# Rotating 96 images by 90 degrees: loads in 1 MB pieces with 32 KB reads over four partitions, middle stores in 32 KB runs

## The chip, the cores and the metric

The kernel runs on one core of a Trainium2 chip. The metric is the device time of one execution in microseconds. Most executions of a kernel agree within 0.3%; a run over 1.5% above the fastest of its kernel is counted as slow and left out of the comparisons. A ratio is the mean time of one kernel's fast runs over the mean of the other's from the same rounds on the same chip, so it is not quite the ratio of the medians that are quoted.

## The reference

```python
def setup_inputs():
    return {"x": np.random.randn(32, 3, 256, 256).astype(np.float32)}   # 25.17 MB

def reference(x):
    return np.rot90(x, k=1, axes=(-2, -1)).astype(np.float32)
```

Every image is turned by a quarter: 25.17 MB are read and as much is written. There is no arithmetic. VectorE transposes small blocks, and the rest of the rotation lies in the access patterns. SyncE and ScalarE do nothing here but issue transfers, each on a queue of its own (q1 and q10 in the profile); 16 DMA engines carry out both queues.

## The kernel before

The data is cut into 24 pieces of 1 MB (4 images each). The first four and last four pieces are handled one by one, the 16 in the middle in four groups of 4 MB. There are 12 slots of 1 MB (8 KB in each of the 128 partitions) for input (`S_all`) and 12 for output (`U_all`).

```python
    AS = [1] * 4 + [4] * 4 + [1] * 4
    for i, a in enumerate(AS):
        s = n % NS                      # NS = 12 slots
        ...
        eng = nc.scalar if i in (1, 3) else nc.sync
        if a == 1:                      # 1 MB: 128 rows of 8 KB, one in each partition
            eng.dma_start(out=S, in_=xg[n].rearrange("(p f) -> p f", p=P))
        else:                           # 4 MB: 128 rows of 32 KB, one in each partition
            eng.dma_start(out=S, in_=xg[n : n + a].rearrange("a (qk f) -> qk a f", f=RI * W))
        ...                             # 1 or 8 nc.vector.transpose
        # stores, always in runs of 8 KB, on ScalarE's queue
        nc.scalar.dma_start(out=og[n : n + a].rearrange("a (p f) -> p a f", p=P), in_=U)
```

The framework places the semaphores: it hands eight DMA completion semaphores round, and a transfer that reuses one waits until the previous transfer on it has landed.

Of the kernel before, what the change touches and what calls it, by code (L numbers as in the profile page):

```python
# [1 line left out]

# [4 lines left out]


@with_exitstack
def kernel(  # L10
    ctx: ExitStack,
    tc: tile.TileContext,
    x: bass.AP,
    out: bass.AP,
):
    nc = tc.nc
    B, C, H, W = x.shape
    assert H == W == 256
    N = B * C
    P = 128  # L20
    R = 8
    F = R * W
    G = N // 4

    AS = [1] * 4 + [4] * 4 + [1] * 4
    assert sum(AS) == G
    NS = NU = 12
    fp32 = mybir.dt.float32

    xf = x.rearrange("b c h w -> (b c h w)")  # L30
    of = out.rearrange("b c h w -> (b c h w)")
    xg = xf.rearrange("(n f) -> n f", n=G)
    og = of.rearrange("(n f) -> n f", n=G)

    S_all = ctx.enter_context(tc.tile_pool(name="S", bufs=1)).tile([P, NS, F], fp32, name="S_all")
    U_all = ctx.enter_context(tc.tile_pool(name="U", bufs=1)).tile([P, NU, F], fp32, name="U_all")

    n = 0
    for i, a in enumerate(AS):
        s = n % NS  # L40
        assert s + a <= NS
        RI = R * a
        S = S_all[:, s : s + a].rearrange("p a f -> p (a f)")
        U = U_all[:, s : s + a]

        eng = nc.scalar if i in (1, 3) else nc.sync
        if a == 1:
            eng.dma_start(out=S, in_=xg[n].rearrange("(p f) -> p f", p=P))
        else:
            eng.dma_start(  # L50
                out=S, in_=xg[n : n + a].rearrange("a (qk f) -> qk a f", f=RI * W)
            )

        src = S.rearrange("p (r k q) -> p q r k", r=RI, q=R)[:, ::-1, :, ::-1]
        dst = U.rearrange("p a (q k r) -> p q r k a", q=R, r=RI)
        if a == 1:
            nc.vector.transpose(dst[:, :, :, :, 0], src)  # L57
        else:
            for q in range(R):
                nc.vector.transpose(dst[:, q], src[:, q])  # L60

        if a == 1:
            nc.scalar.dma_start(out=og[n].rearrange("(p f) -> p f", p=P), in_=U[:, 0])
        else:
            nc.scalar.dma_start(
                out=og[n : n + a].rearrange("a (p f) -> p a f", p=P), in_=U
            )
        n += a


# [1 line left out]
_INS = ['x']  # L72
_OUTS = [((32, 3, 256, 256), 'float32')]


# [23 lines left out]
```

## Time and profile before

| | before |
|---|---|
| median of 4 runs | 123.59 us (123.52 to 123.69) |
| span in the profile | 121.8 us |
| VectorE busy | 94.3 us, 77% |
| DMA packet time, share of 16 engines | 98.2% |

The page's main lines stand in the prediction. The timeline of VectorE before shows how the groups follow each other; columns are start, length of the stretch, engine, line, operation, and in brackets the idle time before it with what ended it:

```profile
24.97 31.70 DVE L60 STREAM_TRANSPOSE U_all<-S_all 128x1024 f32<-128x1024 f32 x16 [1.30 <-DMA S_all<-in_x_dram]
62.83 15.93 DVE L60 STREAM_TRANSPOSE U_all<-S_all 128x1024 f32<-128x1024 f32 x8 [6.15 <-issue]
79.44 15.93 DVE L60 STREAM_TRANSPOSE U_all<-S_all 128x1024 f32<-128x1024 f32 x8 [0.69 <-DVE U_all L60]
```

The first row holds two 4 MB groups back to back. The third group starts at 62.8 us and the fourth at 79.4 us.

### The profile page before, as it was taken

Reading aid. Unit: us, or ns where it says so; the run is one execution under the profiler, and the core shown is the slowest. Engines: PE = TensorE matmul, PEld = TensorE weight load, DVE = VectorE, ACT = ScalarE, POOL = GpSimd, SP = SyncE. Lnnn points to the kernel's source line nnn. Section 1 sums busy time; section 2 is a strip of 40 time slices with the busy share of each in tenths; the row PEclk is TensorE's granted clock in tenths of the full one; section 3 lists DMA queues with packets and bytes.
Section 4 is the critical chain, followed back from the end, with each engine's and each line's share of the span. In section 5 each row is a group of like instructions: output and inputs, shape, how many; then the busy total and the mean of one; then the engine's idle time right before and its main releaser. Section 6 shows DMA issues by size and latency. Waiting matters only on the chain.

```text
span 121.8 us, 127 instructions
## 1 busy us (share of the span) xinstructions
DVE 94.3 (77%) x40; POOL 0.2 (0%) x4
## 2 busy tenths in 40 slices
DVE  0029999779999999996039999899999999993000
POOL 0000000000000000000000000000000000000000
DMA  4999989899989998999899999999999999999995
GB/s 86 409 422 428 549 355 441 347 503 430 430 358 503 430 430 361 511 441 430 315 431 430 430 430 420 431 428 425 428 425 428 428 425 430 430 430 428 428 430 213
DMA packets 4992, 50.33 MB, mean 413 GB/s; under 512 B 384, under 2 KB 384, under 8 KB 384
## 3 DMA queue, kind: packets, MB, share of 16 engines
q10 hardware_dynamic: 3552, 27.26, 53.2%
q1 hardware_dynamic: 1440, 23.07, 45.0%
HBM read 25.17 MB, written 25.17 MB: 413 GB/s over the span
## 4 chain that ended last, share of the span: by engine, by line
DMA 54%; DVE 35%; DVEq 2%; issue 0%
DMA out_dram<-U_all 47%; DVE U_all L57 25%; DVE U_all L60 10%; DMA S_all<-in_x_dram 6%; DVEq L94 2%
## 5 line engine op out<-in xcount | busy, mean ns | idle before, releaser
L60 DVE STREAM_TRANSPOSE U_all<-S_all 128x1024 f32<-128x1024 f32 x32 | 63.6, 2073 | 8.1 <-issue 6.2
L57 DVE STREAM_TRANSPOSE U_all<-S_all 128x2048 f32<-128x2048 f32 x8 | 30.8, 3925 | 8.2 <-DMA S_all<-in_x_dram 8.2
L83 POOL MEMSET const-bfloat16-1.0<- 128x1 bf16 x1 | 0.1, 102 | 0.0
L83 POOL MEMSET const-uint8-127<- 128x1 uint8 x1 | 0.1, 102 | 0.0
L83 POOL MEMSET const-float32-1.0<- 128x1 f32 x1 | 0.1, 99 | 0.0
L83 POOL MEMSET const-float32-0.0<- 128x1 f32 x1 | 0.1, 98 | 0.2 <-issue 0.2
## 6 DMA issues: line engine op xcount, KB each, us to landing
S_all<-in_x_dram SPq DMA_DIRECT2D x4, 4096.0 KB, 24.4
out_dram<-U_all ACTq DMA_DIRECT2D x4, 4096.0 KB, 28.7
out_dram<-U_all ACTq DMA_DIRECT2D x8, 1024.0 KB, 15.1
S_all<-in_x_dram SPq DMA_DIRECT2D x6, 1024.0 KB, 9.7
S_all<-in_x_dram ACTq DMA_DIRECT2D x2, 1024.0 KB, 9.9
```

The source lines that it names most:

```text
L57: nc.vector.transpose(dst[:, :, :, :, 0], src)
L60: nc.vector.transpose(dst[:, q], src[:, q])
L83: nc = _bacc.Bacc("TRN2", target_bir_lowering=False, num_devices=1)
L94: with _tile.TileContext(nc) as tc:
```

## The change

Its intent: larger runs everywhere. Stores of 16 images write 32 KB runs instead of 8 KB. For that, a partition must hold one 8 KB row of each of the four pieces of a group, so middle loads can no longer put 32 KB into one partition. Instead, each 32 KB read is written to four neighbouring partitions, piece by piece, and the loads are meant to be issued 12 pieces ahead. The core of the diff (cut):

```diff
-            eng.dma_start(
-                out=S, in_=xg[n : n + a].rearrange("a (qk f) -> qk a f", f=RI * W)
+            nc.sync.add_instruction(
+                mybir.InstDMACopy(
+                    ...
+                    ins=[nc.sync.lower_ap(xv[n], opt=False)],          # 32 reads of 32 KB
+                    outs=[nc.sync.lower_ap(S_all[:, s], opt=False)],   # 128 partitions, 8 KB each
+                    queue="qSPDynamicHW",
...
-                out=og[n : n + a].rearrange("a (p f) -> p a f", p=P), in_=U
+            out=og[n : n + m].rearrange("b (qk f) -> qk b f", f=R * m * W), in_=U
...
+    with tc.manual_schedule():
+        loaded = 0
+        n = 0
+        for m in MS:
+            while loaded < min(n + NS, G):      # NS = 12
+                load(loaded, loaded % NS)
+                loaded += 1
+            turn(m, n % NS)
+            store(n, m, n % NS)
+            n += m
```

More of the change, by code (lines that the diff above doesn't have):

```diff
@@ L23 @@
     G = N // 4
-    AS = [1] * 4 + [4] * 4 + [1] * 4
-    assert sum(AS) == G
+    MS = [1] * 4 + [4] * 4 + [1] * 4
+    assert sum(MS) == G
     NS = NU = 12
+    FOLD = 32
     fp32 = mybir.dt.float32
@@ L31 @@
     of = out.rearrange("b c h w -> (b c h w)")
-    xg = xf.rearrange("(n f) -> n f", n=G)
+    xp = xf.rearrange("(n p f) -> n p f", n=G, p=P)
+    xv = xf.rearrange("(n d f) -> n d f", n=G, d=FOLD)
     og = of.rearrange("(n f) -> n f", n=G)
@@ L36, with load @@
     U_all = ctx.enter_context(tc.tile_pool(name="U", bufs=1)).tile([P, NU, F], fp32, name="U_all")
-    n = 0
-    for i, a in enumerate(AS):
-        s = n % NS
-        assert s + a <= NS
-        RI = R * a
-        S = S_all[:, s : s + a].rearrange("p a f -> p (a f)")
-        U = U_all[:, s : s + a]
-        eng = nc.scalar if i in (1, 3) else nc.sync
-        if a == 1:
-            eng.dma_start(out=S, in_=xg[n].rearrange("(p f) -> p f", p=P))
-        else:
-            eng.dma_start(
-                out=S, in_=xg[n : n + a].rearrange("a (qk f) -> qk a f", f=RI * W)
-            )
-        src = S.rearrange("p (r k q) -> p q r k", r=RI, q=R)[:, ::-1, :, ::-1]
-        dst = U.rearrange("p a (q k r) -> p q r k a", q=R, r=RI)
-        if a == 1:
-            nc.vector.transpose(dst[:, :, :, :, 0], src)
-        else:
-            for q in range(R):
-                nc.vector.transpose(dst[:, q], src[:, q])
-        if a == 1:
-            nc.scalar.dma_start(out=og[n].rearrange("(p f) -> p f", p=P), in_=U[:, 0])
-        else:
-            nc.scalar.dma_start(
-                out=og[n : n + a].rearrange("a (p f) -> p a f", p=P), in_=U
-            )
-        n += a
+    def load(n, s):
+        if n in (0, 2):
+            nc.sync.dma_start(out=S_all[:, s], in_=xp[n])
+        elif n in (1, 3):
+            nc.scalar.dma_start(out=S_all[:, s], in_=xp[n])
+        else:
+            nc.sync.add_instruction(
+                mybir.InstDMACopy(
+                    name=nc.get_next_instruction_name(),
+                    engine=mybir.EngineType.SP,
+                    ins=[nc.sync.lower_ap(xv[n], opt=False)],
+                    outs=[nc.sync.lower_ap(S_all[:, s], opt=False)],
+                    queue="qSPDynamicHW",
+                    mode="Copy",
+                )
+            )
@@ new lines, in turn, with store @@
+    def turn(m, s):
+        RO = R * m
+        S = S_all[:, s : s + m]
+        U = U_all[:, s : s + m].rearrange("p m f -> p (m f)")
+        src = S.rearrange("p b (r k q) -> p r q k b", r=R, q=RO)[:, :, ::-1, ::-1]
+        dst = U.rearrange("p (q k r) -> p r q k", q=RO, r=R)
+        if m == 1:
+            nc.vector.transpose(dst, src[:, :, :, :, 0])
+        else:
+            for r in range(R):
+                nc.vector.transpose(dst[:, r], src[:, r])
+    def store(n, m, s):
+        U = U_all[:, s : s + m].rearrange("p m f -> p (m f)")
+        nc.scalar.dma_start(
+            out=og[n : n + m].rearrange("b (qk f) -> qk b f", f=R * m * W), in_=U
+        )
@@ L72 @@
+    with tc.manual_schedule():
[5 more added lines that the diff above has]
+                loaded += 1
+            assert n % NS + m <= NS
+            turn(m, n % NS)
+            store(n, m, n % NS)
+            n += m
 _INS = ['x']
```

## The prediction

> **What bounds the kernel now.** I read the page of the kernel before first for its engine shares, because a pure copy-and-transpose has only two candidates: VectorE and the 16 DMA engines.
>
> ```profile
> DVE 94.3 (77%) x40; POOL 0.2 (0%) x4
> ...
> DMA  4999989899989998999899999999999999999995
> ...
> DMA packets 4992, 50.33 MB, mean 413 GB/s; under 512 B 384, under 2 KB 384, under 8 KB 384
> ...
> q10 hardware_dynamic: 3552, 27.26, 53.2%
> q1 hardware_dynamic: 1440, 23.07, 45.0%
> ```
>
> VectorE is busy 77% of the 121.8 us span. The two DMA queues (q1 is issued by SyncE, q10 by ScalarE) hold 53.2 + 45.0 = 98.2% of what 16 engines have: 119.6 us of packet time per engine. The row of slices shows no hole, only a short start and end. So packet time is the bound; the chain of waits, which names stores and transposes in turn, only tells how the work is strung along that busy resource.
>
> Next I asked for the DMA view of two stretches, to get the time of one packet of each size. In 30 to 54 us loads come in 32 KB packets and stores in 8 KB packets; in 96 to 119 us only 8 KB stores run.
>
> ```profile
> DMA packets 570, 10.44 MB, mean 435 GB/s; under 512 B 64, under 2 KB 64, under 8 KB 64
> ...
> q1 hardware_dynamic: 288, 8.39, 81.0%
> q10 hardware_dynamic: 282, 2.05, 20.2%
> ```
>
> ```profile
> DMA packets 1280, 9.83 MB, mean 427 GB/s; under 512 B 80, under 2 KB 80, under 8 KB 80
> ...
> q10 hardware_dynamic: 1280, 9.83, 101.0%
> ```
>
> In the first stretch q1 has 8.39 MB / 32 KB = 256 data packets (the other 32 are 4-byte completion writes), taking 81.0% of 16 x 24 us = 311 us: 1215 ns each. In the second, 1200 data packets take 101.0% of 16 x 23 us = 372 us: 310 ns each. Four 8 KB packets are 1240 ns, so one 32 KB packet saves 25 ns, 2.0%. That is the whole prize in packet size. Also note the split in the first stretch: loads 81.0%, stores 20.2%, that is one 32 KB packet against one 8 KB packet in turn.
>
> Last the groups of VectorE, to see whether it could become the bound.
>
> ```profile
> L60 DVE STREAM_TRANSPOSE U_all<-S_all 128x1024 f32<-128x1024 f32 x32 | 63.6, 2073 | 8.1 <-issue 6.2
> L57 DVE STREAM_TRANSPOSE U_all<-S_all 128x2048 f32<-128x2048 f32 x8 | 30.8, 3925 | 8.2 <-DMA S_all<-in_x_dram 8.2
> ```
>
> It idles 16.3 us in total before its instructions. The timeline has its last row here:
>
> ```profile
> 95.27 15.38 DVE L57 STREAM_TRANSPOSE U_all<-S_all 128x2048 f32<-128x2048 f32 x4
> ```
>
> So VectorE ends at 95.27 + 15.38 = 110.65 us. The last store is then issued and takes 10.3 us to land, where a first 1 MB load with the engines shared takes 7.5 us: it waits behind about 3 MB of backlog. VectorE is thus some 5 us ahead of need.
>
> **What the Trainium skill says.** "DMA: Bandwidth & Descriptors", section "Where 436 GB/s comes from", puts the SBUF port ceiling at 16 x 32 B x 850 MHz = 435.2 GB/s. The trace agrees: 16 x 8192 B / 310 ns = 423 GB/s and 16 x 32768 / 1215 = 432 GB/s. So 32 KB packets are already within 1% of the ceiling; no layout can give much more. The same page, "Why small descriptors are slow (HBM only)", names a fixed overhead of about 3 cycles per packet. The trace has one in kind, 25 / 3 = 8 ns per extra packet, more than the 3.5 ns that 3 cycles at 850 MHz would be; I use the 8 ns. "Queues, rings and completion order" says each engine takes turns between queues packet by packet; the 81.0 to 20.2 split agrees. The fourth place is under rival 4.
>
> On VectorE I rely on the trace alone. The middle transposes exchange the 8 KB step from the write to the read side; the durations per element (3925 / 2048 = 1.92 ns without such a step, 2073 / 1024 = 2.02 ns with it, fixed cost included) hardly differ. I expect no change of VectorE's work.
>
> **The change, part by part.**
>
> Packet counts before. Loads: 8 pieces of 1 MB in 8 KB packets (1024) and 4 of 4 MB in 32 KB packets (512). Stores: 8 x 128 = 1024 at the edges and 4 x 512 = 2048 in the middle, all of 8 KB. Per engine: (512 x 1215 + 4096 x 310) / 16 = 38.9 + 79.4 = 118.2 us. The page has 119.6; the other 1.4 us lies mostly in the first 2 us of packets, which last up to about 1.2 us each in the trace instead of 0.31, and at the changes of stage. The change leaves these first loads alone.
>
> Stores in the middle: 2048 packets of 8 KB become 512 of 32 KB. That saves 512 x 25 ns / 16 = 0.8 us.
>
> Loads: the first 4 stay. The last 4, in 8 KB packets now, get 32 KB reads: 4 x 32 packets, saving at most 128 x 25 / 16 = 0.2 us. The 16 middle pieces read 32 KB as before, but each read now fills four partitions with 8 KB writes. If a packet follows the read, they stay at 1215 ns: nothing. If each 8 KB write costs its 8 ns, the middle loads lose 512 x 25 / 16 = 0.8 us and the last 4 gain nothing, so all cancels. The before trace has no such transfer, so it does not decide; I give the read side 70%.
>
> Completion writes: 36 transfers instead of 24, so 12 more 4-byte packets per engine of 9 ns by the packet records: +0.1 us. Issue of 12 more loads lies on SyncE, 0.36 to 0.5 us each, beside other work.
>
> Sum: -0.8 - 0.2 + 0.1 = -0.9 us in the better case, +0.1 us in the other. Weighted: -0.6 us. The table of stages has one dip:
>
> ```profile
> 57.00:63.00 6.00, 0.17 (x1) 0.00 (x0) 1.00 0.97 395
> 63.00:96.00 33.00, 32.31 (x17) 0.00 (x0) 1.00 1.01 428
> ```
>
> The last column is GB/s: 6 us at 395 instead of 428 lose 0.4 us, when the 4 MB loads ended; a finer queue may get some of that back, so I put the point at -0.8 us: 122.8 us.
>
> This holds only if the engines never run dry. In the built program the eight completion semaphores go round over loads and stores in program order, so "12 pieces ahead" is not what SyncE gets: load 9 waits for the first store to land, load 11 for the second, 12 for the third, 14 for the fourth, 18 for the whole first 16-image store, and 22 for the second. I walked it at 3.04 us per 1 MB load beside 8 KB stores (80% share) and 4.9 us beside 32 KB stores (half share), with 1 us to land. The first middle group is on chip at about 25 us, when VectorE frees at 23.7; load 11 lands at about 40 and VectorE wants it at 42; load 15 at 58.5 and VectorE wants it at 58.6; loads 18 and 19 at 78 against 75 (3 us idle); the last at 98 against 95. VectorE ends at about 110.5, as now. At every moment one of the queues has work, so the engines stay full and the end stays at 119 to 120 us plus the same tail. Waits of SyncE will look long and cost nothing, because a load that is held lets stores run at full rate.
>
> **The rivals.** (1) The turns go the other way: if a widened load counts as 8 KB packets, it gets one turn of 8 KB against a store's 32 KB, a fifth of the rate while a middle store runs. For it: the writes are 8 KB runs. Against: in the before trace the records follow descriptors that are equal on both sides, so nothing can be read. By my walk load 15 would then land near 71 us instead of 58, VectorE would end near 120, and the engines would stand still for some 6 us near 100 us: 127 to 129 us, slower by 3 to 4%. About 7%. (2) A semaphore wait of SyncE leaves VectorE without data at 40 or 58 us, where my margins are only 0 to 2 us. A few us of VectorE idle are covered by the 5 us it is ahead; only more would show. It would make 124 to 126. (3) The transposes slow down by the exchanged step: 10% on 63.6 us is 6.4 us, about the slack, so about 124 to 125; nothing in the profile speaks for it. (4) The widened writes fall on other ports than their engine's. "SBUF — State Buffer", section "Door 1: the DMA port swizzle", has ports in units of four neighbouring partitions, just what one 32 KB read fills, so I hold this unlikely; no run of before shows it. (5) The gain is bigger than packet size: it cannot be, as even 1536 packets of 32 KB at 1215 ns are 116.6 us against 118.2, so 1.6 us or 1.3%.
>
> **Range and chances.** The gain is capped at about 1.6 us, so faster by 2% (2.5 us) needs something not seen here: 3%. Rival 1 and the heavier forms of 2 and 3 make slower by 2%: 8%. The rest, 89%, is within 2%. The range runs from 122.0 (the whole gain and the dip at 60 us) to 124.4 (no gain and a small stall).
>
> **What would show it.** Right: data packets 1536 of 8 KB and 1152 of 32 KB, the latter near 1215 ns also on q1; DMA share again about 98% but of a slightly shorter span; q1 and q10 near equal shares around 50 to 60 us; VectorE means of 2.07 and 3.93 us; VectorE ending near 110 us. Wrong: q1 with 8 KB packets (no load gain), or 32 KB packets of 1240 ns; q1 at a fifth beside middle stores (rival 1); slices under 9 tenths of DMA around 40, 58 or 100 us (rivals 1, 2); a middle transpose over 2.2 us (rival 3); load packets well over 1240 ns (rival 4).

## The result, and the profile after

The changed kernel takes 129.18 us in the median of 4 runs (127.55 to 129.62), before 123.59 us. The ratio is 1.041 (95% interval 1.031 to 1.050): slower by 4%, where 0.7% faster was predicted. Its times also spread more than those of before. The profiled run, at 129.62 us, counts as slow by the rule above; a copy of the kernel in the experiments (the control) shows the same features in a fast run, with one exception that is named there.

The page after, with the rows of engine share, DMA share and GB/s in 40 slices, packets, and the two queues:

```profile
DVE 91.6 (72%) x40; POOL 0.2 (0%) x4
...
DMA  3999899989998989999999999999999939899993
GB/s 105 419 429 527 329 453 453 411 339 517 401 442 355 363 267 411 422 453 401 463 442 401 463 391 411 432 360 411 422 453 411 453 144 483 350 473 375 414 414 134
DMA packets 3264, 50.33 MB, mean 395 GB/s; under 512 B 576, under 2 KB 576, under 8 KB 576
...
q10 hardware_dynamic: 2016, 27.26, 50.5%
q1 hardware_dynamic: 1248, 23.07, 44.7%
```

There are fewer packets, just as meant: 3264 - 576 = 2688 with data, and the trace has 1536 of 8 KB and 1152 of 32 KB. The queues hold 95.2% of 127.4 us = 121.3 us per engine, although the packets were to need less than before (119.6 us). So packets lasted longer, and there is some 4 us more time without packets (127.4 - 121.3 = 6.1 us against 121.8 - 119.6 = 2.2 us; roughly, as records of neighbouring packets can overlap). Two hollows stand out in GB/s: slices 13 to 15 (38 to 48 us) with 355, 363, 267, and slice 33 (102 to 105 us) with 144, where loads and the third big store are done or nearly so and the fourth is issued only at 104.3 us. The row of busy digits hides the first of them: it has 8 or 9 there, as slow packets count as busy.

VectorE's waits (who waited, for what: us in total, times, longest), then its timeline after:

```profile
DVE U_all L71 <- issue: 10.0, 2, 7.6
DVE U_all L71 <- DMA S_all<-in_x_dram: 10.0, 1, 10.0
```

```profile
25.72 30.38 DVE L71 STREAM_TRANSPOSE U_all<-S_all 128x1024 f32<-128x1024 f32 x16 [2.38 <-issue]
66.07 15.28 DVE L71 STREAM_TRANSPOSE U_all<-S_all 128x1024 f32<-128x1024 f32 x8 [9.97 <-DMA S_all<-in_x_dram]
88.98 15.26 DVE L71 STREAM_TRANSPOSE U_all<-S_all 128x1024 f32<-128x1024 f32 x8 [7.63 <-issue]
104.08 15.39 DVE L68 STREAM_TRANSPOSE U_all<-S_all 128x2048 f32<-128x2048 f32 x4
```

VectorE works no longer than before (91.6 us), but stands idle for 10.0 us ahead of the third group and 7.6 us ahead of the fourth. The fourth starts at 89.0 us instead of 79.4, and VectorE ends at 119.5 us instead of 110.65. In this run the last stores have no backlog to hide behind, and the store queue is empty from 103.0 to 105.5 us. That second hollow is the feature that the control lacks.

Why late? SyncE issues the loads in order. Its waits before the change and after it:

```profile
SPq L48 <- DMA out_dram<-U_all: 32.2, 3, 15.7
...
SPq L50 <- DMA out_dram<-U_all: 3.7, 1, 3.7
```

```profile
SPq L49 <- DMA out_dram<-U_all: 57.0, 6, 20.1
...
SPq L49 <- DMA S_all<-in_x_dram: 11.9, 3, 5.7
```

After the change six loads are held until a store lands, 57.0 us in all. No data dependency asks for that: a load needs a free input slot, which the transposes set free, not the stores. The order of waits in the built program gives the list: load 9 waits for the first store, 11 for the second, 12 for the third, 14 for the fourth (1 MB each), 18 and 22 for the first two of 16 images. In the packet records the load queue is empty from 39.9 to 42.0 us; load 12 was issued at 40.4 us, when the third store had landed.

Two more things happen around that point. First, the refill is slow. The stretch table (from and to, length, busy time of VectorE and of GpSimd with counts, granted clock, DMA share, GB/s):

```profile
42.00:48.00 6.00, 6.00 (x4) 0.00 (x0) 1.00 0.98 299
48.00:60.00 12.00, 8.10 (x5) 0.00 (x0) 1.00 1.02 437
```

By their records the engines are busy in both rows, but at 299 GB/s in the first: the 32 KB load packets that start between 42 and 48 us last 1.81 us in the mean instead of 1.21. The first packet of the 16-image store issued at 41.0 us starts only at 46.7 us; from 42.4 us on, when the last 1 MB store was done, the store queue shows no packet at all, so the slow load packets had the engines to themselves.

Second, the loads then crawl. The DMA view of 48 to 60 us:

```profile
DMA packets 195, 5.24 MB, mean 437 GB/s; under 512 B 35, under 2 KB 35, under 8 KB 35
...
q10 hardware_dynamic: 96, 3.15, 60.6%
q1 hardware_dynamic: 99, 2.10, 41.5%
```

Both queues have 32 KB packets, yet they do not share equally: 96 packets of the store stand against 99 - 35 = 64 of loads, 3 to 2. Lining up packets that follow each other without a gap gives the order on one engine (worked out from the records; L and S are 32 KB packets of load and store, l is a load's 4-byte completion write):

```
L S l S L S L S l S L S L S
```

A 1 MB load is two data packets and one completion write per engine, and **the completion write takes a full turn**, for which the store sends another 32 KB. So a piece needs (2 + 3) x 1.213 = 6.07 us, and the trace has loads 13, 14 and 15 landing at 53.80, 59.88 and 65.95 us.

### The profile page after: what moved, and what is told of

It is laid out like the page before. It is cut to its first block, busy times and chain, and to the rows that moved or that the text cites. A ratio compares the mean times of both kernels' runs of the same rounds, so it can differ in the third digit from the quotient of the medians.

```text
span 127.4 us, 147 instructions
## 1 busy us (share of the span) xinstructions
DVE 91.6 (72%) x40; POOL 0.2 (0%) x4
## 2 busy tenths in 40 slices
DMA packets 3264, 50.33 MB, mean 395 GB/s; under 512 B 576, under 2 KB 576, under 8 KB 576
## 4 chain that ended last, share of the span: by engine, by line
DMA 57%; DVE 28%; issue 3%; DVEq 3%; SPq 1%; ACTq 0%
DMA S_all<-in_x_dram 37%; DMA out_dram<-U_all 20%; DVE U_all L71 20%; DVE U_all L68 9%; DVEq L116 3%; SPq L49 1%; ACTq L45 0%
## 5 line engine op out<-in xcount | busy, mean ns | idle before, releaser
L71 DVE STREAM_TRANSPOSE U_all<-S_all 128x1024 f32<-128x1024 f32 x32 | 60.9, 2045 | 20.0 <-issue 10.0
```

Of the source, the lines that this page charges most:

```text
L71: nc.vector.transpose(dst[:, r], src[:, r])
```

## The experiments

All kernels gave the right result. Each was timed in three rounds; "before" was 123.5 to 123.6 us in each of the four calls, which went to different chips. Except for one, they are built from a copy of the changed kernel whose semaphores are placed by hand, one for each load, one for each store, and one that counts the transposed groups. It has the same transfers in the same order on the same queues, and a table of extra waits:

```python
        def load(eng, n):
            if n >= NS:
                eng.wait_ge(dv, turn_of[n - NS] + 1)        # the slot is free: the real dependency
            for kind, j in GATE_L.get(n, []):               # the copied waits, if any
                eng.wait_ge(ld[j] if kind == "L" else st[j], ...)
            ...                                             # the same DMA as in the changed kernel
```

### 1. Control: all copied waits

```diff
+GATE_L = {6: [L1], 7: [L3], 8: [L4], 9: [S0], 10: [L5], 11: [S1], 12: [S2], 13: [L7], 14: [S3],
+          15: [L8], 16: [L10], 17: [L11], 18: [S4], 19: [L12], 20: [L14], 21: [L15, L9], 22: [S5], 23: [L16]}
+GATE_S = {2: [L0], 3: [L2], 4: [L6], 5: [L9], 6: [L13], 7: [L17], 8: [L18], 9: [L19], 10: [S6], 11: [L20]}
```

> Control: the changed kernel with hand-placed semaphores, one per transfer, and with the waits that the changed kernel has on others' landing copied one by one. Every theory expects the changed kernel's time again, 127 to 130 us, with VectorE short of data near 57-66 and 82-89 us. If it comes out near 123 us, the way of placing semaphores itself matters and the next run proves nothing.

Measured: 127.62 us in the median (126.64 to 128.93), ratio 1.030 (1.023 to 1.037). It is as slow as the changed kernel within the spread of both, and its profiled run is a fast one. There the third group starts at 67.87 us and the fourth at 86.96, and 42 to 48 us run at 287 GB/s:

```profile
67.87 15.26 DVE L72 STREAM_TRANSPOSE U_t<-S_t 128x1024 f32<-128x1024 f32 x8 [11.87 <-issue]
86.96 15.26 DVE L72 STREAM_TRANSPOSE U_t<-S_t 128x1024 f32<-128x1024 f32 x8 [3.83 <-DMA S_t<-in_x_dram]
```

So the hand-placed semaphores reproduce the late groups and the slow refill, and what they show of these can be carried over. One feature is missing. The stretch table of the control, and the last stretch in the changed kernel:

```profile
42.00:50.00 8.00, 8.00 (x5) 0.00 (x0) 1.00 0.91 330
62.00:90.00 28.00, 18.29 (x10) 0.00 (x0) 1.00 1.00 404
102.00:106.00 4.00, 4.00 (x3) 0.00 (x0) 1.00 0.99 426
```

```profile
102.00:106.00 4.00, 4.00 (x3) 0.00 (x0) 1.00 0.55 238
```

The hollow near 103 us is in the slow run of the changed kernel and not here. The control still loses most of the time, and its VectorE ends late too (117.45 us). So late data at the end cannot be what makes the control slow; the next run shows what does.

### 2. Copied waits taken away

```diff
-GATE_L = {6: [L1], 7: [L3], ...}
-GATE_S = {2: [L0], 3: [L2], ...}
+GATE_L = {}
+GATE_S = {}
```

> The same with those copied waits removed: a load waits only for the turn that frees its slot, so SyncE really issues up to 12 pieces ahead. Theory A (loads held until a store lands leave the load queue empty, and the refill is slow): the queue never runs dry, the 32 KB load packets that took 1.5 to 2.8 us near 42-47 and 82-86 us vanish, mean load packet back to about 1.22 us, VectorE waits under 8 us after its start, about 122.5 us. Theory B (a load's completion write takes a whole turn beside 32 KB stores, so loads get 2 turns of data in 5): the waits are not the cause; loads beside middle stores still land 6.1 us apart and the time stays at 126 to 129 us. Theory C (a read that fills four partitions is slow in itself): the slow packets stay, wherever stores are absent, 126 us or more.

Measured: 123.21 us (123.06 to 123.24), ratio to before 0.997 (0.995 to 0.998). The same transfers, and 4.4 us less than the control. The DMA rows of its page, and the timeline of VectorE:

```profile
DMA  3999969999899999999999999999999999999995
GB/s 86 421 421 421 551 243 451 473 432 475 367 432 384 459 432 475 421 411 421 432 432 421 443 411 454 411 454 411 454 411 454 411 454 411 454 411 386 430 432 243
```

```profile
25.91 45.34 DVE L71 STREAM_TRANSPOSE U_t<-S_t 128x1024 f32<-128x1024 f32 x24 [2.67 <-DMA S_t<-in_x_dram]
72.54 15.27 DVE L71 STREAM_TRANSPOSE U_t<-S_t 128x1024 f32<-128x1024 f32 x8 [1.29 <-DMA out_dram<-U_t]
```

Three groups now run back to back and the fourth starts at 72.5 us, 16 us earlier than after the change. Both hollows are gone; the mean load packet of 32 KB takes 1.233 us (1.289 after the change). This is Theory A. The first two stretches of the control again, in this run:

```profile
42.00:50.00 8.00, 8.00 (x5) 0.00 (x0) 1.00 1.00 426
62.00:90.00 28.00, 24.97 (x14) 0.00 (x0) 1.00 1.00 431
```

By these rates the control lost about 8 x (1 - 330/426) = 1.8 us and 28 x (1 - 404/431) = 1.75 us. The other 1.7 us of the 5.2 us between the spans (126.5 and 121.3) are an uneven end: the last store's completion writes on the 16 engines come from 123.2 to 125.7 us in the control (half of them by 123.9) and from 119.9 to 120.4 here (half by 120.3). The kernel ends with its slowest engine, so a mean over the 16 does not tell the whole loss.

Note that the 3-to-2 sharing is still there: from 72 to 84 us the DMA view has 96 data packets of the store and 64 of loads. It costs nothing here, where the loads are early.

### 3. Which of the waits: those on 1 MB stores, on 16-image stores, or on loads

Three runs add back one kind each to run 2. All are waits of loads; the waits of stores (`GATE_S`) stay away, and were not tried by themselves.

```diff
 # gate_small_stores
+GATE_L = {9: [S0], 11: [S1], 12: [S2], 14: [S3]}
 # gate_big_stores
+GATE_L = {18: [S4], 22: [S5]}
 # gate_loads_only
+GATE_L = {6: [L1], 7: [L3], 8: [L4], 10: [L5], 13: [L7], 15: [L8], 16: [L10], 17: [L11], 19: [L12], 20: [L14], 21: [L15, L9], 23: [L16]}
```

> own_semaphores with only four of the changed kernel's copied waits: loads 9, 11, 12 and 14 wait until the first, second, third and fourth 1 MB store have landed. Theory A1 (these four drain the load queue near 30-42 us and cause the slow refill): most of the loss comes back, 125.5 to 127.5 us, with slow 32 KB load packets near 42-47 us and the third middle group turned at 63 us or later instead of about 56. Theory A2 (the two waits on 16-image stores are the loss): about 123.3 us.

> own_semaphores with only the other two: loads 18 and 22 wait until the first and second 16-image store have landed. A1: the third group stays at about 56 us; load 18 goes out near 69 us, the fourth group is turned near 82 instead of 72.5 us, which VectorE's lead nearly covers: 123.2 to 124.2 us. A2: 125.5 us or more.

> own_semaphores with all the copied waits of loads on the landing of other loads, and none on stores. Theory A1 (only the waits on stores empty the load queue): a load that waits for an older load still leaves one to four pieces in the queue, so 123.0 to 123.6 us and no slow packets after 30 us. If any copied wait hurts: 125 us or more.

Measured: 129.06 us with the four waits on 1 MB stores, ratio 1.044 (1.041 to 1.047); 124.88 us with the two on 16-image stores, 1.012 (1.008 to 1.016); 123.10 us with all the waits on loads, 0.997 (0.994 to 0.999). The rows, the third group in the first and the fourth group in the second:

```profile
67.95 15.26 DVE L71 STREAM_TRANSPOSE U_t<-S_t 128x1024 f32<-128x1024 f32 x8 [11.15 <-issue]
```

```profile
83.30 15.27 DVE L71 STREAM_TRANSPOSE U_t<-S_t 128x1024 f32<-128x1024 f32 x8 [12.12 <-DMA S_t<-in_x_dram]
```

The four early waits alone bring the whole loss back, to the 129 us of the changed kernel: I had expected 125.5 to 127.5, and it is over the control too, which I did not follow up. The two late ones delay the fourth group by 11 us as expected (82 against 72.5), but cost 1.7 us where I expected at most 1. The late group is not the price by itself: in own_cut4 below it starts as late, at 82.25 us, and the time is 123.63. What the profiled run (124.20, the fastest of its four) shows is an uneven end: the last completion writes come from 119.9 to 121.5 us. Waits on other loads are free: in that trace the load queue is never empty for as long as 1 us until the loads are done.

### 4. One wait alone

```diff
+GATE_L = {12: [S3]}      # added to run 2, and to the same kernel with plain 8 KB loads
```

> own_semaphores with one wait added: load 12 waits until the fourth 1 MB store has landed, so the load queue runs empty once. If a refill of the empty queue is what makes widened load packets slow: again 1 to 2 us per engine of excess over 1.21 us a packet just after load 12, third group 5 us or more later than in own_semaphores, 124 to 126 us. If the slow packets of the changed kernel had another source: no excess, 123.2 to 123.8 us.

> The same single wait with plain 8 KB loads, to be read against own_narrow and one_wait_wide by its packets after load 12, not by its total. If the slowness belongs to reads that fill four partitions: 8 KB load packets stay at 0.31 us there. If it belongs to any refill: they too last well over 0.31 us, an excess near 1 us per engine. Total 126 to 129 us by Theory B.

Measured, with wide reads: 126.44 us (126.12 to 127.72), ratio 1.026 (1.020 to 1.031), so this one wait costs 3.2 us over run 2, 0.4 us more than the range I gave allowed for. In its trace load 12 is issued at 42.95 us, the load queue having been empty since 38.1. Its first packet starts at 48.16, 5.2 us later, with nothing but the 16-image store running meanwhile. The DMA view of 43 to 48 us has only the store's queue in it:

```profile
DMA packets 59, 1.93 MB, mean 387 GB/s; under 512 B 0, under 2 KB 0, under 8 KB 0
...
q10 hardware_dynamic: 59, 1.93, 108.2%
```

While this lasts SyncE's next loads take 1.36 to 2.11 us each to issue, where an unhindered one takes 0.47. The last store packets before the loads come in are slow too, 1.9 to 2.4 us. So slow packets are no property of reads that fill four partitions: this time they were stores. They come here, and near 42 and 84 us in the control, while a transfer that was issued on the other queue has not begun.

But such a refill is not always slow. In gate_big_stores the load queue has no packet from 59.5 to 71.2 us. Load 18 is issued at 67.42 us and starts 3.8 us later, and meanwhile the stores run at full rate:

```profile
67.40:71.20 3.80, 3.78 (x3) 0.00 (x0) 1.00 1.00 431
```

The kernel before has one as well: its load queue is empty from 77.3 to 83.0 us, at 427 GB/s. Nor is a burst of issues enough: run 2 issues four loads and a big store from 41.2 to 43.6 us, at 426 GB/s. So the waits cause the loss, but what makes the engines slow after some of them is open.

With plain loads: 124.96 us, against 125.13 for own_narrow below. This half is inconclusive. Plain loads take their turns more slowly early on, so the fourth store had landed (36.1 us) before the load queue ran dry, and the wait held nothing up.

### 5. Packet sizes and turns

One run cuts each middle store of run 2 into four transfers with 8 KB runs, one does that to the control, one gives run 2 plain loads, and one gives the changed kernel itself (with its own semaphores) plain loads.

```diff
 # own_cut4, gated_cut4
-                eng.dma_start(out=dst, in_=U)
+                for j in range(4):
+                    eng.dma_start(out=dst[:, :, j * c : (j + 1) * c], in_=U[:, j * c : (j + 1) * c])
 # own_narrow, narrow_loads
-            InstDMACopy(ins=[xv[n]], outs=[S_all[:, s]], ...)
+            dma_start(out=S_all[:, s], in_=xp[n])
```

> As own_semaphores, and each middle store cut into four transfers of 1 MB with 8 KB runs, so that a turn of the store queue is 8 KB again. Theory B: beside middle stores loads get 2 x 32 KB against 3 x 8 KB, 73% of the bytes and 3.4 us per piece instead of 6.1; if B is the main loss this is 4 us faster than own_semaphores. Theory A: no gain over own_semaphores, but 0.8 us more packet time for the 8 KB stores, so about 123.2 us. Theory C: the slow packets stay.

> gated_control (all copied waits) with the middle stores cut into four 1 MB transfers of 8 KB runs, so that beside a middle store a load gets 2 x 32 KB against 3 x 8 KB. Theory B as helper (the waits hurt because a late load then crawls at 6.1 us per piece beside 32 KB stores): the third group comes 6 to 8 us earlier than in the control, 124 to 125 us. If the slow refill alone makes the loss: no earlier than 63 us and 127 us.

> own_semaphores with all loads in plain 8 KB rows, 32 KB middle stores kept. Theory B (packets and completion writes take equal turns): beside a middle store a load gets 8 turns of 8 KB and one of 4 bytes against 9 turns of 32 KB, about a fifth of the bytes and some 13 us per 1 MB piece; the fourth group is turned about 15 us later than the 72.5 us of own_semaphores and the engines run dry near 100 us: 126 to 128 us. If turns do not matter: own_semaphores' 123.2 plus at most 0.5 us for the smaller packets.

> The changed kernel with one part undone: middle and last loads in plain 8 KB rows, one partition each, all waits as they are. Theory B: a load has 8 turns of 8 KB and one for its completion against 9 of a store's 32 KB, so loads get about a sixth of the bytes (some 14 to 19%) beside middle stores, 13 us per 1 MB piece; the worst of all, 128 to 133 us. Theory C: the slow packets vanish, and if they are the main loss the time falls to about 124 us. Theory A alone expects no change, 127 to 130 us.

Measured: own_cut4 123.63 us, so 32 KB middle stores are worth 0.4 us (ratios to before 1.0007 and 0.9967), if the changed turns beside them cost nothing. gated_cut4 126.62 us, 1.0 us better than the control. Its third group starts at 59.25 us instead of 67.87, as Theory B wants, but the fourth still waits for a load that is held for a big store, and the total barely moves: B is a helper, not the cause. After 50 us its engines run at 428 GB/s up to 122 us; its loss lies in 42 to 50 us (338 GB/s) and in an uneven end (completion writes from 122.0 to 124.4 us).

own_narrow takes 125.13 us, ratio 1.011 (1.008 to 1.015), less than the 126 to 128 I expected. The sharing itself came out as expected: its fourth group starts at 82.72 us, 10 us later than in run 2, and loads 19 and 20 land at 82.50 and 94.81 us, 12.3 us apart. But the engines did not run dry, so the price was 1.9 us.

narrow_loads takes 125.93 us (124.70 to 126.87), ratio 1.016 (1.010 to 1.022). I had expected it to be the worst of all. It is faster than the changed kernel, even with all its waits. Its DMA view of 48 to 60 us does show the bad share for loads:

```profile
q10 hardware_dynamic: 112, 3.67, 70.8%
q1 hardware_dynamic: 218, 1.65, 32.9%
```

But with plain loads the early loads and the small stores take turns of equal size (8 KB against 8 KB), so the small stores land sooner (the third at 31.8 us instead of 40.3), the held loads go out before the load queue is empty, and the excess of load packets over their usual time is 1.5 us per engine instead of 3.3. So undoing part of the change made its waits cheaper. That is an argument from the two traces; I did not isolate it.

### 6. The kernel before, without copied waits

```diff
+ # the transfers of the kernel before, one semaphore each, GATE_L = GATE_S = {}
```

> The kernel before with one semaphore per transfer and no copied waits. If the copied waits cost nothing in the kernel before, 123.3 to 123.7 us, and own_semaphores against this run is what the transfers alone are worth, 0.2 to 0.6 us. If they cost something there too, 122.5 to 123 us, and the transfers alone are worth nothing or less.

Measured: 123.34 us (123.26 to 123.37), ratio to before 0.998 (0.996 to 1.000). The copied waits cost the kernel before next to nothing. Against this run, own_semaphores with 123.21 us shows what the new transfers are worth by themselves: 0.1 us by the medians, 0.2 by the ratios. The two runs are from different calls, so this is hardly more than nothing.

## Why the prediction was wrong

**What held.** DMA packet time is the bound before. The packet counts were right (1536 and 1152), and the read side does decide: load packets on q1 are of 32 KB. VectorE's transposes did not slow down (2.05 and 3.94 us against 2.07 and 3.93). Loads and stores do take turns packet by packet. Rival 1, the flipped turns, did not come: loads had 40% beside a middle store, not a fifth. The sums are right but for one rounding: 6 us at 395 instead of 428 GB/s lose 0.46 us, not 0.4.

**The step that failed** is "This holds only if the engines never run dry", with its conclusion "At every moment one of the queues has work, so the engines stay full" and "a load that is held lets stores run at full rate". I had found all six waits on stores in the built program, and walked them. A queue did have work throughout, and the engines were not full: in the control 42 to 50 us ran at 330 GB/s, where the same transfers without the waits (run 2) had 426. Two assumptions in the walk were wrong.

1. The walk gave a held load its full share of the rate at once, and had no cost for a refill. The load queue ran empty as walked (load 11 landed at 40.4 us, the walk said about 40), but a refill is slow: 42 to 48 us ran at 299 GB/s, and in run 4 the first packet came 5.2 us after the issue. Load 15 landed at 65.95 us instead of 58.5 (2.3 us of this belong to the second point: two more steps of 6.07 instead of 4.9). Taking the waits on stores away (run 2) or leaving only those on loads removes the loss; putting four of them back restores it.
2. I gave loads half the turns beside 32 KB stores, 4.9 us a piece. The completion write takes a turn too, so it is 6.07 us. By itself this is harmless (run 2 has it), but it makes late loads later: loads 18 and 19 landed at 84.3 and 88.8 us instead of 78, the last at 107.0 instead of 98, and VectorE ended at 119.5 us instead of 110.5. That this delay reaches the time is not shown. In the profiled run of the changed kernel it leaves the hollow near 103 us; in the control VectorE ended at 117.45 us, and the loss lies elsewhere.

So the trigger was that of rival 2, "A semaphore wait of SyncE leaves VectorE without data at 40 or 58 us". I had its place right, even the margins of 0 to 2 us. But I priced it by VectorE's idle time, and the runs show the price on the DMA engines. I gave rival 2 a time of 124 to 126 us, and slower by 2%, from whatever rival, only 8%. A walk with margins near zero at two places should have had a far wider range.

**A term that was mis-sized.** For 32 KB middle stores I reckoned 0.8 us; own_semaphores against own_cut4 measured 0.4. I had multiplied packet durations. But records of neighbouring packets overlap: the share of 101.0% in the prediction's second window said so. From start to start on one engine, in the packet records, it is 306 ns for 8 KB (before, 96 to 119 us) and 1209 ns for 32 KB (run 2, 97 to 108 us). Four small packets then cost 4 x 306 - 1209 = 15 ns more, not 25, and 512 x 15 / 16 makes 0.5 us. Some of that is given back: a 32 KB load that fills four partitions has a median of 1.221 us in run 2, 8 ns more than a store's 1.213.

**What stays open.** Why a transfer on an empty queue mostly waits 3.6 to 5.2 us for its first packet while the other queue has work, and why packets meanwhile last up to twice as long in some of these refills and not in others, is not settled. The runs show that the waits on stores bring the loss and where it lies, not what in the DMA path does it.

A version that beats both: run 2, or the one with waits on loads only (123.10 us, 0.34% under before). The gain is small but outside its interval. The better result is that the transfers of the change are not slow in themselves; they became slow together with the shared semaphores.

## What to carry to other kernels

When completion semaphores are handed round over loads and stores together, a load can be held by a store that it has nothing to do with; read the waits in the built program, and give loads and stores semaphores of their own if a load waits for a store. A lookahead in the source promises nothing: building this kernel with 4 pieces ahead instead of 12 gave the same instructions with the same waits. Do not take an emptied DMA queue as free because the other queue has work: near 42 us its refill cost more than everything the larger packets could earn, though other refills in these traces cost nothing. Look at GB/s there, not at the busy share.

## What the Trainium skill lacked or had wrong

- "DMA: Bandwidth & Descriptors", "Queues, rings and completion order": the turns by packet agree, but the page does not say that a transfer's completion write takes a turn of its own. Measured: 96 store packets to 64 load packets, both of 32 KB, because each 1 MB load has 2 data packets and 1 completion write per engine.
- The same page, "Latency and other measured facts", has about 600 ns to the first byte for transfers from SyncE and ScalarE. Measured: at the start of the kernel the first packets come 1.0 us after the issue begins and 0.65 us after it ends, which agrees; on an empty queue beside the other queue's work it is 5.2 us from the issue in run 4 and 3.8 us in gate_big_stores, which the page does not have.
- The same page, "Why a DMA increments its semaphore by 16 and not by 1", treats a shared semaphore as a matter of correctness. No page treats its price when loads and stores share a rotation: 4.4 us of 127.6 here (control against run 2).
- The same page does not give the cost of a read that is wider than the rows it is written to: 1.221 us against 1.213 for 32 KB over four partitions in the steady state.
- The same page, "Why small descriptors are slow (HBM only)": the prediction set its 3 cycles against 8 ns per extra packet. From start to start it is 15 / 3 = 5 ns, nearer to the 3.5 ns estimated from the page (3 cycles at its 850 MHz); here the page was better than my reading.
